# Storing three heads apart in pieces of 116 rows, with their last twelve rows in one DMA

## The chip, the core and the metric

The kernel runs on one core of one Trainium2 chip. Its time is the device time of one launch in microseconds (us), the median of several runs. A core has TensorE (PE) for matrix products, VectorE (DVE), ScalarE (ACT) and GpSimd (POOL) for the rest, SyncE (SP), which here only issues DMAs, and 16 DMA engines that move data between HBM and the core's memory (SBUF, 128 rows). DMAs are issued from three queues: POOL's, SP's and ACT's.

## The reference

Attention over 8 x 12 = 96 heads with 512 queries and keys of 64 numbers each, in float32. The mask lets position i see itself and its ancestors in a binary tree.

```python
mask[i, i] = 1
parent = i
while parent > 0:
    parent = (parent - 1) // 2
    mask[i, parent] = 1
scores = np.einsum('bhqd,bhkd->bhqk', Q, K) * scale
scores = scores + (1 - mask) * (-1e9)
weights = np.exp(scores - np.max(scores, axis=-1, keepdims=True))
weights = weights / (np.sum(weights, axis=-1, keepdims=True) + 1e-10)
return np.einsum('bhqk,bhkd->bhqd', weights, V)
```

## The kernel before

The 96 heads are worked on in 48 pairs. A step `i` of the main loop computes the scores of pair `i` on TensorE (`scores1`, `scores2`), their exponentials on ScalarE, the products with V of pair `i - 1` (`values`), and on VectorE the division by the sums (`norm`, the lines L732 and L734 of the profile), which writes the outputs of the pair into a tile `of`. Such a tile holds eight heads: 128 rows of 8 x 256 float32, and row `p` of head `h` holds the four positions 4p to 4p + 3. In HBM this is one piece of 1,024 bytes. In the second half of the loop, `head(i, a)` pairs head `8 * (i // 4) + i % 4` with the one four further on: step 36 has heads 72 and 76, step 37 has 73 and 77, step 38 has 74 and 78, step 39 has 75 and 79. `norm(i - 1)` runs in step `i`.

All loads but the first, and most stores, are issued by POOL, in the order of the list that `pool_program` builds; `ready` says from which step on an item may go. POOL issues its list in order, each item when the data are there. The outputs go out in stores of eight heads (`out`, 1 MB each), the last eight heads in pieces: heads 88, 89 and 92, 93 by POOL, heads 90 and 94 by SP and ACT in halves of 64 rows, head 91 by SP in halves, head 95 by ACT.

Two heads are taken out of this order. `store_apart`, called at the end of step `APART_AT` = 38, stores heads 72 and 73 from SP, each in a piece of rows 0 to 115 (`APART_ROWS` = 116) and a piece of rows 116 to 127. POOL's store of heads 72 to 79 then holds six heads. Every store is issued by the function `store`, whose DMA stands at L742. A DMA on SP's or ACT's queue signals through one of eight semaphores, which are used in turn; a DMA that takes one up again waits until the DMA that used it before has landed.

Of the kernel before, what the change touches and what calls it, by code (L numbers as in the profile page):

```python
# [118 lines left out]
def kernel(  # L119
# [7 lines left out]
    nc = tc.nc  # L127
    B, H, S, D = Q.shape
    P = nc.NUM_PARTITIONS
# [466 lines left out]
    def scores1(i):  # L596

        sp = psS.tile([P, 2, 512], fp32, name="s1")
        for a in range(2):
            nc.tensor.matmul(  # L600
                out=sp[:, a, :],
                lhsT=(k1code if i < WIDE else k1wide)[64 * a:64 * a + CODE_ROWS, :],
                rhs=(q1code, q1wide, q1far)[(i >= WIDE) + (i >= FAR)][64 * a:64 * a + CODE_ROWS],
                start=True, stop=False,
            )
        for a in range(2):
            nc.tensor.matmul(  # L607
                out=sp[:, a, :], lhsT=keys(i, a, TOP),
                rhs=qTs[i][64 * a:64 * a + 64, :, :].rearrange("p t c -> p (t c)"),
                start=False, stop=True,  # L610
            )
        et = etpool.tile([P, 2, 4, 128], bf16, name="e1")
        nc.scalar.activation(  # L613
            out=et[:, :, :, :].rearrange("p a t c -> p (a t c)"),
            in_=sp[:, :, :].rearrange("p a c -> p (a c)"),
            func=AF.Exp, scale=scale,
        ) if i < WIDE else nc.scalar.activation(  # L617
            out=et[:, :, :, :].rearrange("p a t (r u) -> p a (t r) u", u=2 if i < FAR else 4),
            in_=sp[:, :, :].rearrange("p a (u c) -> p a c u", u=2 if i < FAR else 4),
            func=AF.Exp, scale=scale,  # L620
        )
        ets[i] = et
# [34 lines left out]
    def scores2(i):  # L657
        if i >= WIDE:
            return scores2_wide(i)
        sp = psS.tile([P, 2, 4, 128], fp32, name="s2")  # L660
        flat = sp[:, :, :, :].rearrange("p a t c -> p a (t c)")
        for a in range(2):
            nc.tensor.matmul(
                out=sp[:, a, :, 32:128], lhsT=k2code[64 * a:64 * a + CODE_ROWS, :],
                rhs=q2code[64 * a:64 * a + CODE_ROWS, :].rearrange(
                    "p (t c) -> p t c", t=4
                )[:, :, 32:128],
                start=True, stop=False,
            )
        for t, lo, hi in ((2, 32, 192), (0, 192, 256), (3, 288, 448), (1, 448, 512)):  # L670
            for a in range(2):
                nc.tensor.matmul(
                    out=flat[:, a, lo:hi], lhsT=keys(i, a, TILE2[t]),
                    rhs=qTs[i][64 * a:64 * a + 64, :, :].rearrange("p t c -> p (t c)")[:, lo:hi],
                    start=False, stop=t == 1, skip_group_check=t in (2, 3),
                )
        nc.scalar.activation(
            out=e2s[i % NE][:, :, :, 32:128].rearrange("p a t c -> p (a t) c"),
            in_=sp[:, :, :, 32:128].rearrange("p a t c -> p (a t) c"),
            func=AF.Exp, scale=scale,  # L680
        )
# [59 lines left out]
    def store(eng, h0, n, step=1, p0=0, p1=P):  # L741
        return eng.dma_start(  # L742
            out=Or[p0:p1, h0:h0 + step * (n - 1) + 1:step, :],
            in_=ofs[h0 // 8][p0:p1, h0 % 8:h0 % 8 + step * (n - 1) + 1:step, :, :].rearrange(
                "p h t d -> p h (t d)"
            ),
        )


    APART, APART_AT, APART_ROWS = 72, 38, 116  # L750

    def store_apart():

        for p0, p1 in ((0, APART_ROWS), (APART_ROWS, P)):
            for h in range(2):
                store(nc.sync, APART + h, 1, 1, p0, p1)

    def pool_program():

        ops = [  # L760
            (load_k, 2, 2), (load_q, 2, 2), (load_v, 0, 4), (load_v, 4, 4),
            (load_k, 4, 2), (load_k, 6, 2), (load_q, 4, 2), (load_k, 8, 4),
            (load_q, 6, 2), (load_q, 8, 4), (load_v, 8, 8), (load_k, 12, 4),
            (load_q, 12, 4), (load_k, 16, 4), (load_rows, 1, "upper"),
            (load_q, 16, 4), (load_rows, 1, "even"), (load_k, 20, 4), (load_rows, 1, "odd"),
            (load_q, 20, 4), (load_k, 24, 8), (load_q, 24, 4), (load_rows, 2, "upper"),
            (load_q, 28, 4), (load_rows, 2, "leaves0", "leaves1"), (load_k, 32, 8), (load_q, 32, 8),
            (load_rows, 3, "upper"),
            (spread_pool, (1, "Z0", 8, 16), (1, "Z1", 8, 16), (1, 6, 8, 16), (1, 9, 8, 16)),
            (load_q, 40, 8), (load_k, 40, 8), (load_rows, 3, "leaves0", "leaves1"), (load_k, 48, 8),  # L770
            (spread_top, 2), (spread_pool, (2, "Z0", 0, 16), (2, "Z1", 0, 16)), (load_q, 48, 8),
            (spread_pool, (2, "X", 0, 16), (2, "M", 0, 16), (2, "D1", 0, 16)), (spread_top, 3, 0, 12),
            (load_rows, 4, "upper"), (spread_top, 3, 12, 16),
        ]
        def tops(o):
            return [(spread_top, o), (spread_pool, (o, "Z0", 0, 16), (o, "Z1", 0, 16))]

        def rest(o):
            return [(spread_pool, (o, "X", 0, 16), (o, "M", 0, 16), (o, "D1", 0, 16))]

        def out(h0, n=KB):
            return [(store, nc.gpsimd, h0, n)]

        def leaves(o):
            return [(load_rows, o, "leaves0", "leaves1")]

        def qk(h0):
            return [(load_k, h0, KB)], [(load_q, h0, KB)]

        k7, q7 = qk(56)  # L790
        k8, q8 = qk(64)
        k9, q9 = qk(72)
        k10, q10 = qk(80)
        k11, q11 = qk(88)
        ops += k7 + q7 + leaves(4) + out(0)
        ops += k8 + q8 + [(spread_pool, *[(3, part, 0, 16) for part in ("Z0", "Z1", "X", "M", "D1")])]
        ops += leaves(5) + [(load_rows, 5, "upper")]
        ops += k9 + tops(4) + q9 + rest(4) + out(8)
        ops += k10 + q10 + out(16)
        ops += k11 + tops(5) + q11 + rest(5)  # L800
        ops += [(lay_beside, "kst", 80 // KB), (lay_beside, "qst", 80 // KB)]
        for h in range(24, 56, KB):
            ops += out(h)
        ops += [(lay_beside, "kst", 88 // KB), (lay_beside, "qst", 88 // KB)]
        for h in range(56, NH - KB, KB):
            n = 2 if h == APART else 0
            ops += out(h + n, KB - n)
        ops += [(store, nc.gpsimd, NH - KB + h, 2) for h in (0, 4)]
        return ops
# [93 lines left out]
    for i in range(NP + 1):  # L903
        steps = FIRST[i] if i < len(FIRST) else "SVK" if i % 2 else "SVQ"
        if i >= max(FAR, KFAR - 4):
            steps = ("SVK", "SVQ", "SVK", "SQV")[i % 4]
        elif i == FAR - 1:
            steps = "SQVK"
        for step in steps:
            if step == "S" and i < NP:  # L910
                scores1(i)
                scores2(i)
            if step == "V" and i >= 1:
                values(i - 1)
                norm(i - 1)
                valued = True
            if step == "K" and kdone < NP:
                kdone = turn("kst", kdone)
            if step == "Q" and qdone < NP:
                qdone = turn("qst", qdone)  # L920
            if step == "W":
                nc.scalar.copy(
                    out=codes[64:64 + CODE_ROWS, 1280:1536], in_=codes[0:CODE_ROWS, 1280:1536]
                )
            if step == "X":
                spin("s1" if valued else "ob", 2)
            if step == "D":
                spread_by(nc.vector.tensor_copy, BY_VECTOR, STEADY_VECTOR, i)
            if step == "A":
                spread_by(nc.scalar.copy, BY_SCALAR, STEADY_SCALAR, i)  # L930
        if "D" not in steps:
            spread_by(nc.vector.tensor_copy, BY_VECTOR, STEADY_VECTOR, i)
        if "A" not in steps:
            spread_by(nc.scalar.copy, BY_SCALAR, STEADY_SCALAR, i)
        pool(i)
        if i == APART_AT:
            store_apart()
        if i == NP - 1:
            for p in (0, P // 2):
                for a, eng in enumerate((nc.sync, nc.scalar)):  # L940
                    store(eng, head(i - 1, a), 1, 1, p, p + P // 2)
# [34 lines left out]
```

## Time and profile before

| | |
|---|---|
| Median of three runs | 132.81 us (132.63 to 132.86) |
| The profiled execution's own time | 133.31 us |
| Its span, from the first instruction to the last | 131.5 us |
| TensorE busy | 114.3 us (87%) |
| VectorE busy | 105.1 us (80%) |
| ScalarE busy | 101.1 us (77%) |
| GpSimd busy | 84.8 us (64%) |
| Written to and read from HBM | 12.58 MB and 37.94 MB |

The page shows the span in 40 slices of 3.29 us. A line `DMA` gives the mean busy share of the 16 DMA engines in tenths, a line `GB/s` what they moved. The view of windows gives the same numbers for any stretch, the view of DMA queues the packets of each queue in it: q0 is POOL's queue, q1 SP's, q10 ACT's, q8 fetches instructions. A packet of POOL's stores has 4,096 bytes, one of SP's and ACT's 1,024 (a row of a head); each DMA ends with a small packet of 4 bytes on every engine that it uses, which signals its completion. In the timeline, the time of a DMA is that of its issue, not of its transfer.

### The profile page before, as it was taken

Reading aid. Unit: us, or ns where it says so; the run is one execution under the profiler, and the core shown is the slowest. Engines: PE = TensorE matmul, PEld = TensorE weight load, DVE = VectorE, ACT = ScalarE, POOL = GpSimd, SP = SyncE. Lnnn points to the kernel's source line nnn. Section 1 sums busy time; section 2 is a strip of 40 time slices with the busy share of each in tenths; the row PEclk is TensorE's granted clock in tenths of the full one; section 3 lists DMA queues with packets and bytes.
Section 4 is the critical chain, followed back from the end, with each engine's and each line's share of the span. In section 5 each row is a group of like instructions: output and inputs, shape, how many; then the busy total and the mean of one; then the engine's idle time right before and its main releaser. Section 6 shows DMA issues by size and latency. Waiting matters only on the chain.

```text
span 131.5 us, 5436 instructions
## 1 busy us (share of the span) xinstructions
PE 114.3 (87%) x2353; PEld 81.2 (62%) x2353; DVE 105.1 (80%) x254; ACT 101.1 (77%) x163; POOL 84.8 (64%) x116
## 2 busy tenths in 40 slices
PE   6787978999899889899999998999899899999600
PEld 2453755777676668677676776767677667756500
DVE  3429769888999998898998998998999979864600
ACT  4269585989799997779995987978898677989500
POOL 6999624445494999995796799927999756002400
PEclk9999999999999999999999999999999999999985
DMA  3999999999999999999999999999999999999991
GB/s 97 242 175 191 202 194 202 199 205 204 201 204 207 208 205 206 208 211 203 209 210 270 302 213 203 205 218 334 239 305 274 265 399 396 397 400 406 376 355 66
DMA packets 26071, 32.25 MB, mean 245 GB/s; under 512 B 1240, under 2 KB 19544, under 8 KB 26048
## 3 DMA queue, kind: packets, MB, share of 16 engines
q0 software_dynamic: 24384, 30.41, 111.0%
q1 hardware_dynamic: 944, 0.91, 2.2%
q10 hardware_dynamic: 720, 0.59, 1.4%
q8 instruction: 18, 0.29, 0.8%
q14 instruction: 5, 0.04, 0.1%
HBM read 37.94 MB, written 12.58 MB: 384 GB/s over the span
## 4 chain that ended last, share of the span: by engine, by line
DVE 28%; PE 28%; DMA 24%; ACT 9%; issue 5%; POOL 2%; ACTq 0%; POOLq 0%
DMA qst<-in_Q_dram 12%; DVE of L734 10%; PE ob L695 10%; DMA kst<-in_K_dram 8%; DMA vst<-in_V_dram 5%; DVE vt L373 4%; ACT e L651 4%; PE s L600 3%; DVE qq L576 3%; ACT e L617 3%; DVE kk L520 3%; DVE rec L732 3%; DVE kk L524 3%; PE s L607 2%; PE qtp L571 2%
## 5 line engine op out<-in xcount | busy, mean ns | idle before, releaser
L617 ACT ACTIVATE e<-s 128x1024 bf16<-128x1024 f32 x40 | 40.9, 1022 | 12.7 <-PE s L607 12.3
L695 PE MATMUL ob<-vt,e 128*128 128x65 bf16 (+1 forms) x940 | 37.5, 197 | 2.3 <-DVE of L734 1.0
L373 POOL COPY vt<-vst 32x512 int32<-32x512 int32 (+4 forms) x44 | 32.8, 745 | 5.3 <-PE ob L695 3.1
L695 PEld LDWEIGHTS <-e 128*128 128x128 bf16 (+1 forms) x960 | 30.2, 102 | 9.6 <-DVE of L734 2.5
L651 ACT ACTIVATE e<-s 128x384 bf16<-128x384 f32 x80 | 34.7, 490 | 0.0
L734 DVE TENSOR_TENSOR of<-ob,rec 128x512 f32<-128x512 f32 x47 | 32.5, 692 | 1.6
L373 DVE COPY vt<-vst 32x1024 bf16<-32x1024 bf16 (+5 forms) x47 | 20.4, 435 | 3.0 <-DMA vst<-in_V_dram 2.2
L742 POOL DMA_DIRECT2D out_dram<-of x13 | 11.3, 875 | 11.0 <-DVE of L734 10.8
L732 DVE RECIPROCAL rec<-ob 128x8 f32<-128x8 f32 x47 | 9.6, 203 | 9.1 <-PE ob L695 8.5
L600 PE MATMUL s<-far,codes 40*128 40x512 bf16 x64 | 12.5, 386 | 0.0
L613 ACT ACTIVATE e<-s 128x1024 bf16<-128x1024 f32 x8 | 8.2, 1022 | 4.5 <-PE s L607 4.4
L634 PEld LDWEIGHTS <-codes 40*128 40x128 bf16 x80 | 6.2, 94 | 8.6 <-issue 3.9
L256 POOL DMA_DIRECT2D qst<-in_Q_dram x12 | 8.5, 706 | 4.7 <-DMA qst<-in_Q_dram 2.5
L576 DVE COPY qq<-qtp 128x1024 bf16<-128x1024 bf16 x16 | 10.9, 682 | 0.4 <-PE qtp L571 0.4
L634 PE MATMUL s<-far,codes 40*128 40x384 bf16 x64 | 10.7, 324 | 0.5 <-ACT e L651 0.3
L373 ACT COPY vt<-vst 32x512 int32<-32x512 int32 (+3 forms) x19 | 10.4, 545 | 0.8 <-DMA vst<-in_V_dram 0.4
L256 POOL DMA_DIRECT2D kst<-in_K_dram x11 | 8.0, 731 | 4.2 <-PE s L645 1.7
L301 POOL DMA_DIRECT2D vst<-in_V_dram x7 | 5.8, 821 | 7.3 <-DMA vst<-in_V_dram 4.4
L645 PEld LDWEIGHTS <-kk 64*128 64x128 bf16 x192 | 8.4, 94 | 2.6
L607 PE MATMUL s<-qq,kk 64*128 64x512 bf16 x48 | 9.2, 378 | 0.2
L520 DVE COPY kk<-ktp 128x256 bf16<-128x256 bf16 x24 | 9.0, 415 | 0.0
L645 PE MATMUL s<-qq,kk 64*128 64x160 bf16 (+1 forms) x192 | 8.9, 208 | 0.0
(64 smaller groups left out, 177.6 us busy)
## 6 DMA issues: line engine op xcount, KB each, us to landing
out_dram<-of POOLq DMA_DIRECT2D x10, 1024.0 KB, 12.8
kst<-in_K_dram POOLq DMA_DIRECT2D x9, 512.0 KB, 16.0
qst<-in_Q_dram POOLq DMA_DIRECT2D x8, 512.0 KB, 14.4
vst<-in_V_dram POOLq DMA_DIRECT2D x12, 256.0 KB, 13.6
vst<-in_V_dram POOLq DMA_DIRECT2D x6, 512.0 KB, 12.9
qst<-in_Q_dram POOLq DMA_DIRECT2D x6, 256.0 KB, 12.1
kst<-in_K_dram POOLq DMA_DIRECT2D x4, 256.0 KB, 10.7
out_dram<-of POOLq DMA_DIRECT2D x1, 768.0 KB, 15.5
```

Source lines behind the costliest of these rows:

```text
L256: return nc.gpsimd.dma_start(out=kept[b][:, h0 % KB:h0 % KB + n, :, :].rearrange("p (g x) t d -> p g (x t d)", x=x), in_=src[:, h0 // x:(h ...
L373: return copy(out=dst, in_=src)
L520: nc.vector.tensor_copy(out=columns(flat, 32 * unit, (640, 4), (step, 2), (4, 8), (1, 4)), in_=columns(kp, base, (256, 4), (128, 2), (1, 8 ...
L576: nc.vector.tensor_copy(out=qqs[j][:, :, 8 * last:8 * last + 8, :].rearrange("p b u c -> p b (u c)"), in_=quarters,)
L600: nc.tensor.matmul(out=sp[:, a, :], lhsT=(k1code if i < WIDE else k1wide)[64 * a:64 * a + CODE_ROWS, :], rhs=(q1code, q1wide, q1far)[(i >= ...
L617: ) if i < WIDE else nc.scalar.activation(
L634: nc.tensor.matmul(out=flat[:, a, :, :].rearrange("p u (t c) -> p u t c", t=4)[:, :, :, 32 // n:], lhsT=k2wide[64 * a:64 * a + CODE_ROWS, ...
L645: nc.tensor.matmul(out=flat[:, a, :, lo:hi], lhsT=keys(i, a, WTILE2[t]), rhs=qT[64 * a:64 * a + 64, :, lo:hi], start=False, stop=t == 1, s ...
L651: nc.scalar.activation(out=e2s[i % NE][:, a, :, 32:128].rearrange("p t (r u) -> p t r u", u=n), in_=flat[:, a, :, :].rearrange("p u (t r) ...
L695: nc.tensor.matmul(out=ob[lo:hi, a, 65 * t:65 * t + 65], lhsT=e[:, a, PLACE[t], lo:hi], rhs=vt[vtile[tile_v][0]][:, head(i, a) % VB, vtile ...
L732: nc.vector.reciprocal(out=rec[:, a:a + n, :, :], in_=o4[:, a:a + n, :, D:D + 1])
L734: nc.vector.tensor_tensor(out=ofs[j][:, h0:h1 + 1:head(i, 1) - head(i, 0), :, :], in0=o4[:, a:a + n, :, 0:D], in1=rec[:, a:a + n, :, :].to ...
```

## The change

Three heads are stored apart, 72, 73 and 74 (`APARTS` = 3). Their rows 0 to 115 still go out in one DMA a head, from SP; the first two at the end of step 38, the third at the end of step 39, since `norm(38)` writes head 74. Rows 116 to 127 of all three heads go out in one DMA behind it, in place of one a head. POOL's store of this group holds five heads in place of six. Nothing else is changed.

```diff
-    APART, APART_AT, APART_ROWS = 72, 38, 116
+    APART, APARTS, APART_AT, APART_ROWS = 72, 3, 38, 116
 
-    def store_apart():
+    def store_apart(i):
 
-        for p0, p1 in ((0, APART_ROWS), (APART_ROWS, P)):
-            for h in range(2):
-                store(nc.sync, APART + h, 1, 1, p0, p1)
+        if i == APART_AT:
+            for h in range(APARTS - 1):
+                store(nc.sync, APART + h, 1, 1, 0, APART_ROWS)
+        if i == APART_AT + 1:
+            store(nc.sync, APART + APARTS - 1, 1, 1, 0, APART_ROWS)
+            store(nc.sync, APART, APARTS, 1, APART_ROWS, P)
...
         for h in range(56, NH - KB, KB):
-            n = 2 if h == APART else 0
+            n = APARTS if h == APART else 0
             ops += out(h + n, KB - n)
...
         pool(i)
-        if i == APART_AT:
-            store_apart()
+        store_apart(i)
```

On SP's queue, these are all DMAs from the loads of the codes to the end; `of` is the tile of outputs and `out_dram` the result in HBM, with rows x heads x numbers behind it:

```order
 L193 DMA codes<-tree_codes 8x1536
-L742 DMA out_dram<-of 116x256 x2
-L742 DMA out_dram<-of 12x256 x2
+L742 DMA out_dram<-of 116x256 x3
+L742 DMA out_dram<-of 12x3x256
 L742 DMA out_dram<-of 64x256 x4
```

One of the two twelve-row stores has become a third store of 116 rows, and the other has three heads in it. The number of DMAs on SP is the same.

On POOL, these are the last stores, from heads 56 to 71 on:

```order
 L742 DMA out_dram<-of 128x8x256 x2
-L742 DMA out_dram<-of 128x6x256
+L742 DMA out_dram<-of 128x5x256
 L742 DMA out_dram<-of 128x8x256
 L742 DMA out_dram<-of 128x2x256 x2
```

The store of heads 72 to 79 has one head less; nothing has moved past another. With their waits, SP's stores of the kernel after the change read so (a name DMAHW is one of the eight semaphores, DVE_49 that of VectorE):

```order
L742 DMA out_dram<-of 116x256 [waits DVE_49] x3
L742 DMA out_dram<-of 12x3x256 [waits DMAHW0_49]
L742 DMA out_dram<-of 64x256 [waits DMAHW2_49,DVE_49]
L742 DMA out_dram<-of 64x256 [waits DMAHW4_49]
L742 DMA out_dram<-of 64x256 [waits DMAHW5_49,DVE_49]
L742 DMA out_dram<-of 64x256 [waits DMAHW7_49]
```

The semaphores 5, 6 and 7 are those of the first three stores of the group in either kernel. Before, the third was the twelve rows of head 72; now it is the 116 rows of head 74, and the last row here waits for it.

## The prediction

> **What bounds the kernel now.** I read the page first, then the end of the chain of waits, then the stores' issues, then the DMA queues window by window. The page's slices and the last row of the chain come first.
>
> ```profile
> span 131.5 us, 5436 instructions
> DMA  3999999999999999999999999999999999999991
> GB/s 97 242 175 191 202 194 202 199 205 204 201 204 207 208 205 206 208 211 203 209 210 270 302 213 203 205 218 334 239 305 274 265 399 396 397 400 406 376 355 66
> ...
> 124.83 0.42 DVE of L734
> ```
>
> The last computing instruction ends at 124.83 + 0.42 = 125.25 us and the span at 131.5 us: the last 6.25 us are stores alone. The rate jumps to about 400 GB/s from slice 33 (105 us) and stays there: from there on the 16 DMA engines work through a backlog of stores. The last two stores are issued at 126 us:
>
> ```profile
> 126.03 0.54 ACTq L742 DMA_DIRECT2D out_dram<-of  x1
> 126.09 0.77 SPq L742 DMA_DIRECT2D out_dram<-of  x1
> ```
>
> How the backlog drains is seen in the view of windows; its last two columns are the DMA engines' busy share and GB/s. The first row is a stretch in which all 16 are full, the others are the end.
>
> ```profile
> 119.50:122.00 2.50, 2.37 (x45) 1.45 (x42) 1.58 (x3) 2.30 (x5) 0.00 (x0) 1.00 1.04 410
> ...
> 127.50:128.00 0.50, 0.00 (x0) 0.00 (x0) 0.00 (x0) 0.00 (x0) 0.00 (x0) 0.50 0.96 340
> 128.00:128.50 0.50, 0.00 (x0) 0.00 (x0) 0.00 (x0) 0.00 (x0) 0.00 (x0) 0.50 0.74 258
> 128.50:129.00 0.50, 0.00 (x0) 0.00 (x0) 0.00 (x0) 0.00 (x0) 0.00 (x0) 0.50 0.48 170
> 129.00:129.25 0.25, 0.00 (x0) 0.00 (x0) 0.00 (x0) 0.00 (x0) 0.00 (x0) 0.50 0.27 90
> 129.25:129.50 0.25, 0.00 (x0) 0.00 (x0) 0.00 (x0) 0.00 (x0) 0.00 (x0) 0.50 0.21 70
> 129.50:129.75 0.25, 0.00 (x0) 0.00 (x0) 0.00 (x0) 0.00 (x0) 0.00 (x0) 0.50 0.14 49
> 129.75:130.00 0.25, 0.00 (x0) 0.00 (x0) 0.00 (x0) 0.00 (x0) 0.00 (x0) 0.50 0.14 49
> 130.00:130.25 0.25, 0.00 (x0) 0.00 (x0) 0.00 (x0) 0.00 (x0) 0.00 (x0) 0.50 0.06 21
> 130.25:131.50 1.25, 0.00 (x0) 0.00 (x0) 0.00 (x0) 0.00 (x0) 0.00 (x0) 0.50 0.00 0
> ```
>
> Sixteen times the share is the number of engines still at work: 15 at 127.75, 12 at 128.25, 8 at 128.75, 4 at 129.1, 3 at 129.4, 2 from 129.5 to about 130.1. So two engines set the end, some 0.6 us behind the third last and 1.5 to 2 us behind most. What a row costs an engine is read here too. With two engines left, 49 GB/s is 24.5 GB/s each, so 1,024 bytes take 41.8 ns; in the full stretch 410 GB/s over 16 is 25.6 GB/s, so a packet of 4,096 bytes takes 160 ns. The question is what the change does to the engines that are last.
>
> **Which engines carry the heads stored apart.** Here is the view of DMA queues for three stretches (packets, MB, share of 16 engines): 104 to 124 us, 113 to 115 us, and 124 us to the end. q1 is SP's queue, q10 ACT's, q0 POOL's.
>
> ```profile
> q1 hardware_dynamic: 288, 0.26, 3.8%
> ...
> q0 software_dynamic: 201, 0.77, 98.0%
> q1 hardware_dynamic: 41, 0.04, 5.9%
> ...
> q0 software_dynamic: 349, 1.23, 41.8%
> q1 hardware_dynamic: 320, 0.26, 10.6%
> q10 hardware_dynamic: 304, 0.26, 10.4%
> ```
>
> Up to 124 us SP's queue moves 256 rows (2 x 116 + 2 x 12) and 32 small packets, 16 for each head: one small packet per engine and DMA tells of its completion. In the tail it is 256 rows and 64, so 16 engines for each 64-row store. For the 41 packets in 2 us there is this reading: an engine with both queues full alternates one row with one POOL packet, 42 + 160 = 202 ns a turn, so one engine does 9.9 rows in 2 us, and 41 are four engines. Hence the 116-row stores lie on four engines, 29 rows each, and the 12-row stores, with the other 12 completions, on twelve engines, one row each; the four are among the twelve, since the last small packets of SP's queue follow the four's own rows.
>
> The Trainium skill, DMA: Bandwidth & Descriptors, section "Why a DMA increments its semaphore by 16 and not by 1", says that such a DMA runs on the largest count up to 16 that divides its rows, on the lowest-numbered engines. For 116 and 12 rows that gives 4 and 12, and the trace agrees (41 packets in 2 us, 16 completions a head). Its rule table has "Use all 16 engines" and so speaks against the change; if the 116 rows were spread over 16, the sum below would be 0 in place of +0.31 us.
>
> Per head that is moved from POOL's queue, each of the four gains 29 rows and loses 8 (two POOL packets), and the other twelve only lose. Before, the four have 2 x 29 + 2 = 60 rows on SP's queue. So are the two last engines among the four? I followed the rings of the four packet by packet. Where POOL's store of a head group completes on one of them, its small packet takes POOL's turn, and the next row comes 48 ns after the last in place of 202. The view of queues in three short stretches shows the latest of the four: a completion at 116.80 to 116.82 (one small packet, one row), its next completion at 119.72 to 119.74, and the end of an engine at 129.52 to 129.56 (one row and one small packet of SP's queue).
>
> ```profile
> DMA packets 4, 0.01 MB, mean 461 GB/s; under 512 B 1, under 2 KB 2, under 8 KB 4
> ...
> DMA packets 1, 0.00 MB, mean 0 GB/s; under 512 B 1, under 2 KB 1, under 8 KB 1
> ...
> DMA packets 2, 0.00 MB, mean 26 GB/s; under 512 B 1, under 2 KB 2, under 8 KB 2
> ```
>
> From 119.73 this engine has POOL's stores of 16 + 12 + 16 + 4 + 4 = 52 packets to do (8, 6, 8, 2 and 2 heads) and the 32 rows of the last stores: 52 x 160 ns + 32 x 41.8 ns + some completions = 8.32 + 1.34 + 0.1 = 9.76, so 129.5 us, where the number of engines falls from 3 to 2. The other three, at the completions 118.99, 119.32 and 119.36 by the same reading, end at about 128.8, 129.1 and 129.15. The two last are others. Two completions lie in the stretch 124.84 to 124.90, 0.6 us and more behind the four (119.73 + 28 x 160 ns = 124.2):
>
> ```profile
> DMA packets 12, 0.04 MB, mean 683 GB/s; under 512 B 2, under 2 KB 2, under 8 KB 12
> ...
> DMA packets 3, 0.00 MB, mean 10 GB/s; under 512 B 2, under 2 KB 3, under 8 KB 3
> ```
>
> From 124.85 there remain 24 packets and 32 rows, 3.84 + 1.34 + 0.1 = 5.3 us: 130.13 to 130.17. The second row is the stretch 130.10 to 130.20, with the last two completions of all. So the two late engines are of the twelve, late from before the stretch, and the four have at most 0.6 us of room behind them.
>
> The Trainium skill, same page, section "Latency and other measured facts", says that DMA engines 7 and 15 are usually slower than the rest under POOL's queue. That fits two late engines outside the lowest four; the trace here carries no engine numbers, so no run so far shows it.
>
> **The change, part by part.**
>
> - *Head 74 leaves POOL's queue.* Each engine loses 8 KB there: 2 packets x 160 ns = 0.32 us on all 16. POOL's own instruction gets shorter and hides nothing new; its wait is the same, for the last pair of heads 72 to 79.
> - *Its 116 rows go to the four engines.* 29 x 41.8 ns = 1.21 us on each. Both bounds lie near: a row could cost at the least nothing, if the four stood idle somewhere, and at the most 202 ns, if POOL's turn were lost with it. The four show no gap between 107 us and the end by the sum above, and POOL's packet in the turn is work that is due anyway; I take 41.8.
> - *The last twelve rows in one DMA.* Three rows on each of twelve engines in place of two: one row more, 0.04 us, on the four and on eight others; one completion less. On SP the two 12-row issues took these two rows:
>
> ```profile
> 105.34 0.92 SPq L742 DMA_DIRECT2D out_dram<-of  x1
> ...
> 106.30 1.04 SPq L742 DMA_DIRECT2D out_dram<-of  x1
> ```
>
>   One of them goes, but SP then waits until 123.94 us for its next store, so it saves nothing at the end. If the single one took twice 1.04 us, it would still end by 110 us.
> - *The third 116-row store waits for head 74.* That head is normalised one step later (the row below ends at 107.71 us), so SP issues it there, and the twelve rows behind it. The rings of the four are at SP's rows until 118 to 119.4 before, so the new rows queue behind them without a gap, whatever the 2.7 us; the cover is 10 us long.
>
> ```profile
> 107.02 0.69 DVE L734 TENSOR_TENSOR of<-ob,rec 128x512 f32<-128x512 f32 x1
> ```
>
> - *A wait.* SP's last store waits for the completion of the third DMA of this group (a shared semaphore): before, of twelve rows; now, of head 74's 116 rows. Their last comes at about 107 + 82 x 0.202 + 5 x 0.048 = 123.8 us, 2.3 us ahead of that store's issue at 126.09. Behind it only the end of the program waits. Costed at nothing; if it is later than 126.1, the price is rival 3's.
>
> Sum for the four: + 1.21 + 0.04 - 0.32 = + 0.93 us, so their ends go from 128.8, 129.1, 129.15, 129.53 to 129.75, 130.05, 130.1, 130.46. Sum for the two late engines: - 0.32 + 0.04 = - 0.28 us, or - 0.32 where no row of the twelve falls: 129.85. The end moves from 130.15 to 130.46, + 0.31 us. The profiled execution took 133.31 us (span 131.5 and 1.8 around it), 0.50 above the median of the runs, 132.81; on the median it is 133.12.
>
> **Rivals.**
>
> 1. *The two late engines stay last, and are relieved* (faster). It holds if in the timed runs the latest of the four ends 0.31 + 0.28 = 0.6 us earlier against them than in the profile. For it: the latest of the four is 0.4 us behind its three neighbours, which is not made by the change. Against: its lag is there at 116.8 already and nothing later can catch it up. The time: 132.81 - 0.30 = 132.5.
> 2. *It balances* (no change). If the latest of the four ran with the other three, the four would end at 130.1 against 130.15 before: - 0.05 us, 132.76. Or if its lag is half as large, + 0.1.
> 3. *The four are last already in the timed runs* (slower by more). The timed runs are 0.5 us shorter than the profiled one; if that is the two late engines' lag, the whole 0.93 us is added: 133.74. A late completion on SP's last store would add here too: for each us past 126.1 up to 1 us at the end.
> 4. *The change moves nothing*: if the third head's rows were spread over all 16 engines, the load would be the same: 132.81. The 41 packets speak against it.
>
> **How the numbers follow.** About 0.2%, 0.27 us, is what a measurement of this kernel can tell from no change. The forecast (+ 0.1 to + 0.6 around + 0.31) has 0.50; 0.40 of it lies above 0.27 and 0.10 below. Rival 1 has 0.18, rival 2 0.14, rival 3 0.14, rival 4 0.04. Slower: 0.40 + 0.14 = 0.54; same: 0.10 + 0.14 + 0.04 = 0.28; faster: 0.18. The forecast's own range is 132.9 to 133.4. The range of 8 in 10 takes in most of rival 1 and of rival 3: 132.52 to 133.70.
>
> **What would show it.** In the changed profile: SP's queue with 348 + 36 rows and 12 + 12 completions between 104 and 126 us, at 40 packets in 2 us, ending near 124.5 and not 119.4; between 129.5 and 130.0 four engines or more at work in place of two, and one alone at 130.4. Right on the rows but wrong on the end would be a drain that ends at 129.85 with two engines (rival 1). The forecast is wrong if the third head's rows run on more than four engines, if SP's last store is issued later than 126.1, or if the two late engines turn out to be among the four.

## The result and the profile after

The changed kernel took 133.86 us (133.31 to 134.58), the kernel before 133.14 beside it: a ratio of 1.0053, with a 95% interval of 1.003 to 1.0076. That is + 0.71 us (+ 0.40 to + 1.0) where + 0.31 was forecast, and 133.86 lies above the forecast range. A second comparison gave 133.49 against 132.80, a ratio of 1.0039 (1.0016 to 1.0062), or + 0.5 us (+ 0.2 to + 0.8); its interval still holds the + 0.31.

The profiled execution of the kernel after took 133.71 us. From its page, the span and the slices:

```profile
span 131.8 us, 5433 instructions
DMA  3999999999999999999999999999999999999983
GB/s 97 238 185 192 201 195 200 201 204 204 201 204 209 206 207 205 209 211 203 209 210 278 298 212 200 208 223 342 225 318 260 274 401 396 398 402 382 374 309 97
```

The last computing instruction and the last stores in its timeline:

```profile
125.46 2.93 SPq L742 DMA_DIRECT2D out_dram<-of  x4
125.46 2.64 ACTq L742 DMA_DIRECT2D out_dram<-of  x3
...
126.34 0.42 DVE L734 TENSOR_TENSOR of<-s,rec 128x256 f32<-128x256 f32 x1
```

SP's queue in the kernel after, from 104 to 126 us and from 113 to 115 us (packets, MB, share of 16 engines):

```profile
q1 hardware_dynamic: 408, 0.39, 5.1%
...
q1 hardware_dynamic: 49, 0.05, 6.6%
```

The 408 packets are the 348 + 36 rows and 12 + 12 completions that were forecast, and 49 packets in 2 us, where 40 were forecast, still are four engines that take a row and a packet of POOL in turn (four of the 49 are completions of SP). The drain of the kernel after, to be set against the same view of before:

```profile
128.50:129.00 0.50, 0.00 (x0) 0.00 (x0) 0.00 (x0) 0.00 (x0) 0.00 (x0) 0.50 0.95 285
129.00:129.25 0.25, 0.00 (x0) 0.00 (x0) 0.00 (x0) 0.00 (x0) 0.00 (x0) 0.50 0.82 275
129.25:129.50 0.25, 0.00 (x0) 0.00 (x0) 0.00 (x0) 0.00 (x0) 0.00 (x0) 0.50 0.73 246
129.50:129.75 0.25, 0.00 (x0) 0.00 (x0) 0.00 (x0) 0.00 (x0) 0.00 (x0) 0.50 0.33 111
129.75:130.00 0.25, 0.00 (x0) 0.00 (x0) 0.00 (x0) 0.00 (x0) 0.00 (x0) 0.50 0.14 49
130.00:130.25 0.25, 0.00 (x0) 0.00 (x0) 0.00 (x0) 0.00 (x0) 0.00 (x0) 0.50 0.07 25
130.25:130.50 0.25, 0.00 (x0) 0.00 (x0) 0.00 (x0) 0.00 (x0) 0.00 (x0) 0.50 0.07 25
130.50:131.20 0.70, 0.00 (x0) 0.00 (x0) 0.00 (x0) 0.00 (x0) 0.00 (x0) 0.50 0.00 0
```

One engine alone is at work from 130.0 us, and its last packet ends at 130.54 us; 130.46 was the sum for the latest of the four engines with the 116-row stores. That it is this engine shows at SP's last rows ahead of the final stores. The two views are of queues, from 125.24 to 125.28 us and from 130.45 to 130.60 us:

```profile
DMA packets 6, 0.02 MB, mean 410 GB/s; under 512 B 2, under 2 KB 2, under 8 KB 6
q0 software_dynamic: 5, 0.02, 106.9%
q1 hardware_dynamic: 1, 0.00, 1.4%
...
DMA packets 3, 0.00 MB, mean 14 GB/s; under 512 B 1, under 2 KB 3, under 8 KB 3
q1 hardware_dynamic: 3, 0.00, 4.2%
```

At 125.26 us comes the last completion of the twelve rows of three heads, on the latest of the four, some 5.3 us ahead of the last packet of all. Followed packet by packet (the section "Fourth" below says how), this engine has 24 packets of POOL and 32 rows left behind it, the same work for which the prediction counted 5.3 us from 124.85 us on, and its end is the last packet at 130.54.

The compute ends at 126.76 us, 1.5 us later than in before's profile (125.25). What delayed it lies ahead of the first store that the change alters: VectorE's copy L373 at 104.33 us took 1.24 us in place of 0.42, beside POOL's copy L447 of 104.23 us, after POOL had come to its stores 0.7 us later. One profile of the kernel before (before_third, below) shows the same late end of the compute, and one of the kernel after (after_fifth) the early one; whether the change makes the late end more frequent is taken up below.

In the eight profiles of the kernels before and after, the execution's time less the end of its last packet is 3.0 to 3.3 us, so the end of the last packet is the quantity to follow. Over all twenty profiles of this study it is 3.0 to 3.6; the most, 3.56 and 3.59, stand with early_119 and four_119 and were not explained.

### The profile page after: what moved, and what is told of

Its sections match the earlier page's. It is cut to its first block, busy times and chain, and to the rows that moved or that the text cites. A ratio compares the mean times of both kernels' runs of the same rounds, so it can differ in the third digit from the quotient of the medians.

```text
span 131.8 us, 5433 instructions
## 1 busy us (share of the span) xinstructions
PE 113.8 (86%) x2350; PEld 81.3 (62%) x2353; DVE 107.2 (81%) x254; ACT 101.1 (77%) x163; POOL 84.4 (64%) x116
## 3 DMA queue, kind: packets, MB, share of 16 engines
q1 hardware_dynamic: 1064, 1.04, 2.5%
## 4 chain that ended last, share of the span: by engine, by line
DVE 42%; PE 24%; DMA 17%; POOL 6%; issue 4%; ACT 3%; ACTq 0%; DVEq 0%; POOLq 0%
DMA vst<-in_V_dram 17%; DVE of L734 13%; PE ob L695 10%; DVE vt L373 9%; DVE rec L732 4%; DVE qq L576 4%; DVE kk L520 4%; DVE kk L524 3%; PE s L600 3%; POOL kst L246 2%; PE qtp L571 2%; POOL qst L246 2%; PE s L607 2%; PE s L634 2%; ACT e L651 2%
## 5 line engine op out<-in xcount | busy, mean ns | idle before, releaser
L373 POOL COPY vt<-vst 32x512 int32<-32x512 int32 (+4 forms) x44 | 32.5, 739 | 6.9 <-PE ob L695 4.7
L373 DVE COPY vt<-vst 32x1024 bf16<-32x1024 bf16 (+5 forms) x47 | 22.5, 478 | 2.9 <-DMA vst<-in_V_dram 2.0
L373 ACT COPY vt<-vst 32x512 int32<-32x512 int32 (+3 forms) x19 | 10.4, 545 | 0.5
L571 PE MATMUL qtp<-ptile,qst 128*64 128x128 bf16 x192 | 7.9, 221 | 1.8 <-DVE qq L576 0.9
```

What stands on the lines that cost most here:

```text
L373: return copy(out=dst, in_=src)
```

## The experiments

Each row compares with runs of the kernel before beside it, with the 95% interval of the ratio. The last column is the end of the last packet in the profiled execution, which is one draw: that of two_even took 134.75 us, 0.6 above its median, and that of three_119, 133.14, was the shortest of its twelve.

| run | what | us | ratio | last packet, us |
|---|---|---|---|---|
| one_head | head 72 apart | 133.52 | 1.0018 (0.9995 to 1.0041) | 130.00 |
| two_joined | two heads, last twelve rows in one DMA | 133.01 | 0.9980 (0.9957 to 1.0004) | 130.18 |
| two_119 | two heads, 119 + 9 rows | 133.18 | 0.9981 (0.9952 to 1.0010) | 129.72 |
| two_late | two heads, one step later | 133.04 | 1.0000 (0.9982 to 1.0017) | 129.64 |
| two_even | two heads, 112 + 16 rows | 134.17 | 1.0080 (1.0050 to 1.0109) | 131.58 |
| three_mixed | two heads 116 + 12, a third whole | 133.23 | 0.9995 (0.9975 to 1.0015) | 130.17 |
| three_115 | three heads, 115 + 13 | 133.64 | 1.0044 (1.0023 to 1.0065) | 130.40 |
| three_119 | three heads, 119 + 9 | 133.45 | 1.0043 (1.0024 to 1.0062) | 129.88 |
| three_even | three heads, 112 + 16 | 134.00 | 1.0052 (1.0023 to 1.0080) | 130.91 |
| early_119 | three heads, 119 + 9, all at step 38 | 134.03 | 1.0073 (1.0048 to 1.0099) | 130.40 |
| four_119 | four heads, 119 + 9 | 134.38 | 1.0095 (1.0067 to 1.0123) | 130.81 |

### First: the parts of the change

Theory L is the prediction's own: an engine's end is its packets of POOL times 160 ns and its rows times 41.8 ns, the four engines carry the rows, and two late engines without them set the end. Theory F in the expectations is the prediction's rival 3: the four are last in the kernel before too.

One head apart (the number of heads in `store_apart` and `n` in `pool_program`):

```diff
-            for h in range(2):
+            for h in range(1):
...
-            n = 2 if h == APART else 0
+            n = 1 if h == APART else 0
```

> Only head 72 is stored apart (116 rows and 12 rows), head 73 stays in POOL's store. The four engines carry 29 + 1 rows on SP's queue in place of 60 and get two POOL packets back: - 30 x 41.8 ns + 0.32 = - 0.93 us; the other twelve get + 0.28 to + 0.32 us. Theory F (in the usual execution the four are already last in the kernel before): faster, by 0.3 to 0.9 us, depending on how close the two late engines follow. Theory L (the two late engines of the twelve are last before, as in the profile shown): slower by 0.28 us.

Measured + 0.18%, an interval from nothing to + 0.4%, with + 0.28 us forecast by L: it fits, but does not exclude no change. Theory F, by which this run is 0.3 to 0.9 us faster, falls.

Two heads, with the joined DMA alone:

```diff
-        for p0, p1 in ((0, APART_ROWS), (APART_ROWS, P)):
-            for h in range(2):
-                store(nc.sync, APART + h, 1, 1, p0, p1)
+        for h in range(2):
+            store(nc.sync, APART + h, 1, 1, 0, APART_ROWS)
+        store(nc.sync, APART, 2, 1, APART_ROWS, P)
```

> The kernel before with one part of the change alone: the last twelve rows of heads 72 and 73 in one DMA, two rows on each of twelve engines as before. Theories F and L both: no change, within 0.1 us. If joining the twelve rows is itself what costs (theory J), it is slower by much of the 0.7 us measured.

No change: the joined DMA costs nothing.

The changed kernel with other pieces, and the kernel before with other pieces:

```diff
-    APART, APARTS, APART_AT, APART_ROWS = 72, 3, 38, 116
+    APART, APARTS, APART_AT, APART_ROWS = 72, 3, 38, 112
```

> The kernel after, but in pieces of 112 and 16 rows, both of which divide by 16: the three heads still go out on SP's queue, and their rows lie on all 16 engines, 24 on each. Against the kernel before the four lose 36 rows and two POOL packets, - 1.83 us, and the twelve get + 0.60 us. Theory L: slower by 0.6 us. Theory F: between - 0.3 and + 0.3 us. If the third head on SP's queue costs by itself, wherever its rows lie: + 0.7 us or more against before, as the kernel after, and the sum of rows on the four would not matter.

```diff
-    APART, APART_AT, APART_ROWS = 72, 38, 116
+    APART, APART_AT, APART_ROWS = 72, 38, 119
```

> The kernel before with pieces of 119 and 9 rows: by its divisors 119 rows go to seven engines, 17 rows each, 9 rows to nine. The four carry 34 + 2 rows in place of 60, - 1.0 us; three or more others get the 34 rows (+ 1.4 us). Theory F: faster by 0.3 to 0.9 us. Theory L: 0 if the two late engines are not among the seven, slower by more than 0.6 us if one of them is.

Both fit L: + 0.5% with rows on all engines, nothing with 36 rows on each of seven. The + 0.5% also lies outside F's - 0.3 to + 0.3 us.

### Second: where theory L fell

Three heads in pieces of 119 and 9 rows put 54 rows on seven engines in place of 90 on four, and by L that is less than the 60 of the kernel before.

```diff
-    APART, APARTS, APART_AT, APART_ROWS = 72, 3, 38, 116
+    APART, APARTS, APART_AT, APART_ROWS = 72, 3, 38, 119
```

> The kernel after with pieces of 119 and 9 rows: three heads on SP's queue as in the kernel after, their rows on seven engines, 54 each, in place of 90 on four. The late two keep their relief of 0.28 to 0.32 us against the kernel before, if they are not among the seven; the four have 6 rows and two POOL packets less than before, - 0.57 us. Theory L: 0.3 us faster than before, and so 0.7 us or more faster than the kernel after. If the third head costs by its number, its later issue, the longer DMA of the last rows or the wait of SP's last store, and not by the rows on the four: as slow as the kernel after, + 0.7 us.

It was slower by 0.43%, as slow as the changed kernel. A fourth head (75, one step later again) made it worse:

```diff
-    APART, APARTS, APART_AT, APART_ROWS = 72, 3, 38, 116
+    APART, APARTS, APART_AT, APART_ROWS = 72, 4, 38, 119
...
-            for h in range(APARTS - 1):
+            for h in range(2):
                 store(nc.sync, APART + h, 1, 1, 0, APART_ROWS)
         if i == APART_AT + 1:
+            store(nc.sync, APART + 2, 1, 1, 0, APART_ROWS)
+        if i == APART_AT + 2:
             store(nc.sync, APART + APARTS - 1, 1, 1, 0, APART_ROWS)
             store(nc.sync, APART, APARTS, 1, APART_ROWS, P)
```

> Four heads (72 to 75) in pieces of 119 rows, the last nine rows of all four in one DMA, head 75 issued one step later. The late two lose another head: - 0.6 us against the kernel before; the seven carry 72 rows, the four 12 more than before and four POOL packets less, - 0.14 us. Theory L: 0.4 to 0.6 us faster than before if the seven do not become last, 0.1 us faster if they do.

Slower by 0.95% where L forecast a gain. Both kernels were profiled again:

> The kernel after, once more, with a second profile. Theory L (the late two last before, the four last after): 0.31 us slower than before by the sum made on one profile, and one to four engines at the end that had rows of SP's queue up to about 124.5 us. Theory F (the four last in both): 0.9 us slower.

> The kernel before, for a second profile of it. Theory L: again two engines alone at the end, the four that carry the heads apart 0.3 to 0.9 us ahead of them. Theory F: the four are last.

The second comparison of the kernel after, + 0.5 us (+ 0.2 to + 0.8), holds L's + 0.31 and not F's + 0.9; its profile ends at 130.38 us. The second of before took 132.86 us, near its median, and its drain is this:

```profile
128.50:129.00 0.50, 0.00 (x0) 0.00 (x0) 0.00 (x0) 0.00 (x0) 0.00 (x0) 0.50 0.46 156
129.00:129.25 0.25, 0.00 (x0) 0.00 (x0) 0.00 (x0) 0.00 (x0) 0.00 (x0) 0.50 0.28 98
129.25:129.50 0.25, 0.00 (x0) 0.00 (x0) 0.00 (x0) 0.00 (x0) 0.00 (x0) 0.50 0.15 49
129.50:129.75 0.25, 0.00 (x0) 0.00 (x0) 0.00 (x0) 0.00 (x0) 0.00 (x0) 0.50 0.07 25
129.75:130.00 0.25, 0.00 (x0) 0.00 (x0) 0.00 (x0) 0.00 (x0) 0.00 (x0) 0.50 0.00 0
```

Its last packet ends at 129.79, 0.37 us ahead of the profile that the prediction used, in an execution 0.45 us shorter. How much of that is the lag of the late engines is read below, where the engines are followed.

### Third: does the time or the number of the heads cost?

If three heads cost wherever their rows lie, it may be that the third comes later (theory A), or that each head taken out of POOL's store costs by itself (theory B).

```diff
-    APART, APART_AT, APART_ROWS = 72, 38, 116
+    APART, APARTS, APART_AT, APART_ROWS = 71, 3, 38, 119
...
-            for h in range(2):
+            for h in range(APARTS):
...
-            n = 2 if h == APART else 0
-            ops += out(h + n, KB - n)
+            n = 2 if h == APART + 1 else 0
+            ops += out(h + n, KB - n - (h + KB - 1 == APART))
```

> Three heads on SP's queue again, in pieces of 119 and 9 rows, but the third is head 71, which is finished already: all three are issued together at the step at which the kernel before issues two. Its last nine rows go by three DMAs. If the third head costs because it is issued 3 to 4 us later than the other two (theory A), the time is that of two heads in the same pieces: 132.8 to 132.9 on a before of 132.8. If it costs by the number of heads taken out of POOL's queue or put on SP's, whenever that is (theory B), it is slower by as much as three heads in these pieces were before: + 0.4 to + 0.6 us. By the count of packets and rows alone (theory L: the late two engines end 0.32 us earlier) it is faster by 0.3 us.

```diff
-    APART, APART_AT, APART_ROWS = 72, 38, 116
+    APART, APART_AT, APART_ROWS = 72, 39, 116
```

> Two heads, 116 and 12 rows as in the kernel before, but both issued one step later, when the third head of the changed kernel is. Theory A (the later issue costs): + 0.4 to + 0.6 us. Theories B and L: no change within 0.2 us, since the rows of SP's queue still end by about 122 us, ahead of the last stores.

Theory A falls twice: two heads one step later cost nothing, and three heads all at step 38 cost 0.73%. Why these cost even more than the three of three_119 was not settled; 0.3 us of it stands behind the last packet (3.56 us against 3.26).

> A second profile of three heads in pieces of 119 and 9 rows; the first was of the shortest of its twelve runs. Theory B: the engines that are last carry few of SP's rows and end at 130.1 or later, later than in both profiles of the kernel before. Theory L: they end 0.3 us earlier than there, at 129.5 to 129.85.

It ended at 130.03 us, in 133.35 us, between the two theories' ranges; one to three engines are at work in the last 0.6 us:

```profile
129.25:129.50 0.25, 0.00 (x0) 0.00 (x0) 0.00 (x0) 0.00 (x0) 0.00 (x0) 0.50 0.17 57
129.50:129.75 0.25, 0.00 (x0) 0.00 (x0) 0.00 (x0) 0.00 (x0) 0.00 (x0) 0.50 0.14 49
129.75:130.00 0.25, 0.00 (x0) 0.00 (x0) 0.00 (x0) 0.00 (x0) 0.00 (x0) 0.50 0.09 29
```

### Fourth: seven engines start late

This trace has no engine numbers, but a packet follows the one ahead of it on its engine with 3 or 4 ns of overlap, and between two of POOL's completions lie 16 packets of a store of eight heads. With both, an engine can be followed through most of the stretch. That showed what L had left out: the engines do not come to the stores together. The last load moves packets of 2,048 bytes, the stores 4,096. The view of queues for before in two stretches, from 101.0 to 102.0 us, with loads alone, and from 104.6 to 105.2 us:

```profile
DMA packets 110, 0.21 MB, mean 209 GB/s; under 512 B 9, under 2 KB 9, under 8 KB 110
...
DMA packets 62, 0.20 MB, mean 331 GB/s; under 512 B 0, under 2 KB 0, under 8 KB 62
```

With loads alone 16 engines move 209 GB/s, with stores alone 410 (119.5 to 122 us). The 331 GB/s at 105 us are (331 - 209) / (410 - 209) = 0.61 of the way: nine or ten engines are at stores, six or seven still at the last load. The completions say the same: in before's profile nine engines end the last load at 103.6 to 104.5 us, and the other seven at 105.4 to 106.4. Nineteen of the twenty profiles show such a gap, with six to eight late engines; in after_fourth the two groups run into each other.

So an engine ends at (end of its last load) + (packets of POOL) x 160 ns + (its rows) x 41.8 ns, plus, where it comes to that, a fetch of instructions: three such packets of 16,384 bytes lie between 104 and 126 us, and each holds one engine for 1.02 to 1.04 us. In before, for the stretch 115.7 to 116.8 us:

```profile
q8 instruction: 1, 0.02, 5.9%
```

That is theory P. It reads the end of each kernel anew:

- *Before*: the engines with the rows left the load early; two of the four could be followed back to it, to 103.9 and 104.0 us. The last engine of all, to 130.16 us, left it at about 106.1, carried at most two rows and took a fetch, most likely the one at 115.7: without one its work would reach back to 107.2 us only, where no load is left.
- *three_119 and three_again*: the last two engines of either carried 54 rows each and left the load at 105.3 to 105.5 us. 105.3 + six stores of eight heads, 15.4, + 54 rows, 2.3, + the rest, 6.9, = 129.9.

The same following, from the last completion of SP's rows on each of the four engines to the end, gives the lag on which the prediction's sum rests. In before the latest of the four ends at 129.54 us and the last engine 0.62 us behind it. In before_again the four end at 128.4, 128.9, 129.0 and 129.27, and the last engine 0.52 us behind them, at 129.79; so most of the 0.37 us between the two profiles is common to both groups. In before_third (below) the latest of the four ends at 129.51, and an engine that has no row of SP after 117.6 us is last, 0.90 us behind. In two_late, with the same rows one step later, the latest of the four ends at 129.49 or later and the last packet at 129.64: a lag of 0.15 us at most. For before_again these are the views of queues of 118.965 to 118.98 us (the last completion of SP's rows on the latest of the four), of 129.258 to 129.27 (its end) and of 129.78 to 129.80 (the last packet of all):

```profile
DMA packets 3, 0.01 MB, mean 342 GB/s; under 512 B 1, under 2 KB 2, under 8 KB 3
q1 hardware_dynamic: 2, 0.00, 22.9%
...
DMA packets 4, 0.00 MB, mean 171 GB/s; under 512 B 2, under 2 KB 4, under 8 KB 4
q1 hardware_dynamic: 2, 0.00, 9.4%
...
DMA packets 1, 0.00 MB, mean 0 GB/s; under 512 B 1, under 2 KB 1, under 8 KB 1
q1 hardware_dynamic: 1, 0.00, 2.8%
```

The Trainium skill, DMA: Bandwidth & Descriptors, section "Latency and other measured facts", has DMA engines 7 and 15 as the usually slower ones, which the prediction took up for its two late engines. The trace has no engine numbers, so it cannot say whether these two are among the late ones; it shows six to eight late engines and not two, and what puts one or two of them behind the others in before is, where it could be followed, a fetch of 1.04 us.

Four runs were to tell P from L and B. First, three heads on five engines:

```diff
-    APART, APARTS, APART_AT, APART_ROWS = 72, 3, 38, 116
+    APART, APARTS, APART_AT, APART_ROWS = 72, 3, 38, 115
```

> Three heads, pieces of 115 and 13 rows: five engines with 23 rows a head, 72 in all, in place of four with 90. By rows alone (theory L) the fullest engine has 18 rows less than in the changed kernel, 0.75 us: 132.9 to 133.1 on a before of 132.8. By the engines' lag (theory P: the fifth engine is one of the seven that leave the last load 2 us late, so that it ends at about 105.5 + 22.3 + 72 x 0.042 = 130.8) it is no faster than the changed kernel: 133.5 to 134.1, with one engine alone at the end, at 130.5 to 131.

133.64 us, + 0.44%: L falls again, since 18 rows less on the fullest engines brought nothing beside the changed kernel. The time is as P forecast it, and one engine alone is at work at the end:

```profile
129.75:130.00 0.25, 0.00 (x0) 0.00 (x0) 0.00 (x0) 0.00 (x0) 0.00 (x0) 1.00 0.06 20
130.00:130.25 0.25, 0.00 (x0) 0.00 (x0) 0.00 (x0) 0.00 (x0) 0.00 (x0) 0.51 0.07 25
130.25:130.50 0.25, 0.00 (x0) 0.00 (x0) 0.00 (x0) 0.00 (x0) 0.00 (x0) 0.50 0.04 12
```

But it ends at 130.40, 0.1 ahead of the forecast 130.5 to 131, and it could not be followed back far enough to say whether it is the fifth engine with a late start or an early one that also took a fetch. So this run bears P's time out, not its reason.

Second, a third head whose rows lie on all engines:

```diff
-            store(nc.sync, APART + APARTS - 1, 1, 1, 0, APART_ROWS)
-            store(nc.sync, APART, APARTS, 1, APART_ROWS, P)
+            store(nc.sync, APART + APARTS - 1, 1)
+            store(nc.sync, APART, APARTS - 1, 1, APART_ROWS, P)
```

> Two heads in pieces of 116 and 12 rows as in the kernel before; the third goes to SP's queue too, but whole, 128 rows over all sixteen engines, 8 rows each, which takes as long as the two packets that POOL's store loses. Theory P: every engine has what it had, no change within 0.2 us. If each head taken out of POOL's store costs by itself (theory B): + 0.4 to + 0.6 us.

0.9995 (0.9975 to 1.0015): no change. Three heads are on SP's queue and POOL's store has five, as in the changed kernel, so theory B falls: what costs is where the rows lie. This is also the case of the prediction's rival 4, a third head spread over all 16 engines, and its zero is borne out.

Third, the kernel before with its rows on all engines:

```diff
-    APART, APART_AT, APART_ROWS = 72, 38, 116
+    APART, APART_AT, APART_ROWS = 72, 38, 112
```

> Two heads in pieces of 112 and 16 rows, which lie on all sixteen engines, 16 rows each, in place of 60 on four and 2 on eight. Theory P: the four get 1.8 us of room that is worth nothing, the late engines get 14 to 16 rows more: + 0.5 to + 0.6 us. If an even spread is what counts: no change or faster.

+ 0.80% (+ 0.50 to + 1.09), more than the + 0.5 to + 0.6 us that P gave. In its profiled execution, 0.6 us longer than its median, two engines are still at work past 130.5 us:

```profile
130.25:130.50 0.25, 0.00 (x0) 0.00 (x0) 0.00 (x0) 0.00 (x0) 0.00 (x0) 0.50 0.14 49
130.50:131.20 0.70, 0.00 (x0) 0.00 (x0) 0.00 (x0) 0.00 (x0) 0.00 (x0) 0.50 0.13 44
```

The Trainium skill, same page, section "Rules for kernel authors", says to use all 16 engines. Here the run goes the other way: the even spread takes 0.80%, 1 us, more than the same two heads with most of their rows on four engines. By P that is because the late engines then carry rows too.

Fourth, the kernel before for its profile:

> The kernel before once more, for its profile. Theory P: the engines that are last are late ones without SP's rows, and they end between 129.6 and 130.2, while the four end at 129.2 to 129.6.

133.46 us, the last packet at 130.41, 0.2 us later than expected. The rest is as P has it: a late engine without SP's rows is last, and the latest of the four ends at 129.51 us. Its compute ends late, at 126.89 us.

### Fifth: within one kind of execution

By then both profiles of the kernel after had late compute, two of three of before had not. If the change only made late compute more frequent (theory R), its four engines would not be the cause.

> The changed kernel again, for its profile. If its four engines set the end (theory P), it ends later than the kernel before in an execution of the same kind: last packet at 130.2 to 130.5 us where the computing ends early (before: 129.8 and 130.2), at 130.4 to 130.6 where it ends late (before: 130.4), with one to three engines at the end. If only the kind of the execution matters (theory R), an execution with early computing ends at 129.8 to 130.2, as before's.

> As the run after_third. Theory R: most executions of the changed kernel are of the later kind. Theory P: both kinds occur, as for the kernel before.

> As the runs after_third and after_fourth: by theory P the last packet lands at 130.2 to 130.6 us in either kind of execution, by theory R at 129.8 to 130.2 us where the computing ends early.

They took 133.49, 134.54 and 133.57 us and ended at 130.35, 131.50 and 130.31 us; the compute ended at 126.07, 127.93 and 125.36 us. In after_fifth the compute ends as early as in before's profile, and its drain still goes on past before's:

```profile
129.50:129.75 0.25, 0.00 (x0) 0.00 (x0) 0.00 (x0) 0.00 (x0) 0.00 (x0) 0.50 0.22 74
129.75:130.00 0.25, 0.00 (x0) 0.00 (x0) 0.00 (x0) 0.00 (x0) 0.00 (x0) 0.50 0.10 33
130.00:130.25 0.25, 0.00 (x0) 0.00 (x0) 0.00 (x0) 0.00 (x0) 0.00 (x0) 0.50 0.06 20
130.25:130.50 0.25, 0.00 (x0) 0.00 (x0) 0.00 (x0) 0.00 (x0) 0.00 (x0) 0.50 0.01 4
```

With early compute, three profiles of two heads in pieces of 116 rows (before, before_again, two_late) end at 130.16, 129.79 and 129.64, this one of three heads at 130.31. One profile of the kernel after is too few to show by its end alone that the change costs within one kind. With late compute, the spans overlap: two_joined, three_mixed and before_third end at 130.18, 130.17 and 130.41, and after, after_again and after_fourth at 130.54, 130.38 and 131.50; after_third, between the kinds, at 130.35.

What decides is which engine is last. Followed back in the same way, the last engine is one that carried SP's rows to 125.0 to 126.2 us in all five profiles of the kernel after (in after_fifth by the likelier of two readings, 2 ns apart), with early and with late compute, and it is none of the four in the three profiles of before. The latest of the four ends at 129.54, 129.27 and 129.51 us before and at 130.54, 130.38, 130.35, 131.50 and 130.31 after. So the four set the end after the change in either kind, and theory R falls as the only cause. Whether the change also makes late compute more frequent is open: five profiles of a kernel don't tell, and the timed runs have none.

No run was clearly faster than the kernel before. two_joined and two_119 lie 0.2% under the kernel before, with intervals that reach past 1.

## Why the prediction was right and wrong

- *The rows.* Right: 348 + 36 rows and 24 completions on SP's queue, four engines for the 116-row pieces, seven for 119, all for 112, 54 rows an engine in three_119.
- *The sum for the four.* Right: + 0.93 us to 130.46; one of the four ends last in all five profiles of the kernel after, and in four of them at 130.31 to 130.54. By the medians of the profiles, 129.51 before and 130.38 after, the latest of the four moved by 0.87 us. In the fifth, at 131.50, SP's rows end 1.0 us later than in after, at 126.23 us; why was not explained.
- *The joined DMA at nothing.* Right (two_joined, 0.9980).
- *The third head one step later at nothing.* Right (two_late, 1.0000).
- *The wait of SP's last store at nothing.* Right in after's profile: the third head's completions come by 125.26 us, SP issued that store at 127.6, later than the 126.1 named, but because the compute ended 1.5 us later. In after_fifth it issued it at 126.7, behind completions that had come by 125.2.
- *Slots and timing on SP's queue.* The rows ended at 125.2 us, 0.7 us later than the 124.5 named; SP's first store was 0.7 us later too.
- *The end before, at 130.15 us, and with it the lag of the late engines: the step that failed.* The sum put the two late engines 0.62 us behind the latest of the four (130.15 against 129.53), let this lag take up all but 0.31 of the 0.93 us, and moved the difference from one profiled execution onto the median. The lag is no fixed quantity: it is 0.62, 0.52 and 0.90 us in the three profiles of before and at most 0.15 in two_late, which has the same rows and the same time. In the timed runs the change cost 0.71 and 0.5 us of the 0.93, so there the lag took up some 0.2 to 0.4 us: this is the mis-sized term. Why it was worth less there than in the three profiles of before is not shown; they are too few for a typical value, and the two measured intervals are wide. The 0.50 us by which the profiled execution exceeded the median is no reason either: against the nine runs beside the changed kernel, 133.14, it was 0.17.
- *Rival 3.* Its 133.74, with a chance of 0.14, came nearest, but by luck: its condition, that the four are last already, does not hold in the three profiles of before, and one_head was not faster.
- *What makes an engine late.* Missed. The prediction had two late engines; there are six to eight that leave the last load about 2 us after the others, and fetches of 1.04 us on single engines. It does not change the sum for the four, which are early ones, but it is where the lag comes from, and why the sum failed for three_119.

What stays open: the lag in the typical execution of the kernel before, why these engines leave the loads late, which engines the fetches fall on, and the sizes of early_119 and two_even, 0.3 us and more above what P gives.

## What to carry to other kernels

When a kernel ends in a drain of stores, its time is that of the last engine, and one profile shows one draw of which engine that is: before the distance between two groups of engines goes into a sum, read it in several profiles. Here 0.62 us in one was 0.90 in another and 0.15 at most in a third. A split of stores over few engines is judged by where each engine stands when the stores begin, not by an even count: here the rows of two heads were free on four early engines and cost when they were spread over all.

## What the runs showed of the hardware

- Sixteen DMA engines left the last load in two groups, about 2 us apart (103.6 to 104.5 us and 105.4 to 106.4 in before).
- A fetch of instructions (16,384 bytes) holds one engine for 1.02 to 1.04 us in the middle of a stream of stores, three times in every execution (at 108.4, 115.7 and 122.1 us in before, within 3 us of these in the others); a 1,024-byte row takes 42 ns there and a 4,096-byte packet about 160.
- VectorE's copy of 32 x 1024 bf16 took 0.42 us in one execution and 1.24 in another, beside the same copy of POOL (1.04 and 1.05 us); where the compute then ended about 1.5 us later, the execution was little longer: 133.46 us against 133.31 and 132.86 for before, 133.71 and 133.42 against 133.57 for after. In after_fourth, with the compute 2.6 us later than in after_fifth, it was 134.54 us.
